# Finer decay steps, earlier decay-row loads and grouped state products in a hybrid DeltaNet/Mamba decoder step

## The chip, the cores and the metric

The kernel runs on one core of a Trainium2 chip. The metric is the device time of one execution in microseconds; the time before is the median of three runs. The engines are TensorE (PE, matmuls; PEld is its weight load), VectorE (DVE), ScalarE (ACT), GpSimd (POOL) and SyncE (SP, which here issues nearly all DMA transfers, in order).

## The reference

One step of a two-layer decoder trunk, for a prompt of 256 tokens and for 8 samples of 4 tokens each that carry states. Layer 0 mixes tokens by a gated DeltaNet, layer 1 by a Mamba-2 scan; each is followed by a SwiGLU network. Cut to what the change touches:

```python
def _gated_delta_rule(q, k, v, g, beta, s0):          # 16 heads of 128
    cum = jnp.cumsum(g, axis=-1)
    seg = cum[..., :, None] - cum[..., None, :]
    decay = jnp.exp(jnp.where(causal, seg, -jnp.inf))
    kk = jnp.einsum('bnhik,bnhjk->bnhij', kb, k) * decay
    tri = jnp.eye(c) + jnp.where(strict, kk, 0.0)
    sol = lax.linalg.triangular_solve(tri, rhs, left_side=True, lower=True, unit_diagonal=True)
    qk = jnp.einsum('bnhik,bnhjk->bnhij', q, k) * decay
    # per block: delta = u - w S;  o = (q e^cum) S + qk delta;  S = e^last S + k_dec^T delta

def _ssd_scan(x, dt, a, bm, cm, h0):                  # 32 heads of 64, 4 groups
    decay = jnp.exp(jnp.where(causal, seg, -jnp.inf))
    cb = jnp.einsum('bnigs,bnjgs->bnijg', cm, bm)
    y_diag = jnp.einsum('bnijg,bnijgr,bnjgrp->bnigrp', cb, decay, xdt)
```

The samples start from `s0 = state_gdn`, so that their k and q are multiplied with 8 x 16 state matrices of 128 x 128.

## The kernel before

All 288 tokens (256 of the prompt, 32 of the samples) lie along the free dimension of x, 128 model columns to a partition block. Every projection is a "dense pair" (`dense_g`, `dense_chunk`): weights of 128 x 1024 come in by one 512 KB DMA from SP into a tile of the tag `raw` (six buffers), ACT rounds them to `wh`, DVE takes the rest as `wl`, and PE multiplies three times (`pd<-hh,wh`, `pd<-hh,wl`, `pd<-hl,wh`). Work is written as generators that yield between steps. `weave` (a planner) takes several generators with a number of steps each and traces them in proportion; a scheduler then puts the instructions of every engine in order, earlier traced work first where it is ready, and each engine runs its own instructions strictly in that order. `burst` traces the first of a list of matmuls and puts the others right behind it at high priority.

The stages that matter here, in the order of time:

- *Decays* (function `gdn`, around L750). The cumulative decays of the prompt's 16 heads are written to DRAM (`cumd`, `cumq`) and read back, repeated over partitions. `D` holds the decays inside blocks of 32 tokens, 128 x 1024: four loads (L753), an add of `nb`, a clamp, one exponential. Behind this exponential, by `issue_after`, come `elS` and `cbs` (the samples' decays, 128 x 512, four clamps and an exponential). This is traced ahead of the first weave (L783), which runs the tasks `k0 q0 k1 k3 q1 k2 q2 q3`: the dense pairs for k and q with their convolutions, and the modulation's matmuls (`mods`). In a convolution, `hist` is a copy by ACT of a transposed piece of the old rows, `kf` is DVE's last step of one block of k. `D` is used only after this weave, when the blocks' triangular matrices are inverted.
- *State products* (`s0_products`, L720 to L743). DVE inverts the blocks in a series of 31 pairs of operations on `X`; beside it run the dense pairs of z and v and, for r = 0 and 1, the products of the samples' k and q (`kms`) with the states. Per batch there is one 512 KB load into a `raw` tile (`s0`, in the trace `s`) and four matmuls of 32 columns (`spa<-s,kms`) into one PSUM tile; the scheduler may put other matmuls between them. A float32 matmul is two instructions.
- *Head pairs* (`pre` and `scan`, L870 to L990). For each pair j of 16 heads, `pre(j)` builds the decays `PP` from `cumd` (two loads of 128 KB at L878, four clamped adds by DVE, an exponential by ACT) and the factors `U`, `Kd`; `scan(j)` runs the two blocks of 128 tokens: products `pe`, `pS`, `po2`, the last of which reads `PP` (`<-ep,PP`). `PP` has two buffers. One weave per pair holds `scan(j)`, `pre(j + 1)` and dense work; `sample` (with `KSQ`) is part of that dense list.
- *Mamba groups* (`core`, L1380 to L1425). Each group of 8 heads is done in four head pairs: DVE multiplies the decays `D` by the products of C and B, and four matmuls of 64 columns (`py<-D,xt`) give the pair's output; they are traced as plain matmuls.

Of the kernel before, what the change touches and what calls it, by code (L numbers as in the profile page):

```python
# [14 lines left out]
P = 128  # L15
# [3 lines left out]
NB = 8  # L19
# [8 lines left out]
def tile_hybrid_step(ctx: ExitStack, tc: tile.TileContext, I, O):  # L28
# [527 lines left out]
    def gdn(gt1, nrm):  # L556
# [165 lines left out]
        def s0_products(r, km):  # L722

            for h in range(2):
                for x_ in range(2):
                    o = 512 * h + 16 * (h if x_ == 0 else 1 - h)
                    G.tensor_copy(
                        km[:, o:o + 528].rearrange("p (b y) -> p b y", y=132)[:, :, 0:128].rearrange(  # L730
                            "p b (q t) -> p b q t", q=4)[:, :, :, 0:4],
                        kqs[:, r, x_, :, 16 * h:16 * h + 16].rearrange("p q (b t) -> p b q t", t=4))
            pa = pss.tile([P, 2, 256], F32, tag="s", name="spa")
            for b in range(NB):
                s0 = raw_tile("s0")
                SY.dma_start(s0.rearrange("p (h v) -> p h v", h=8),
                             I["state_gdn"][0, b, 8 * r:8 * r + 8].rearrange("h k v -> k h v"))
                for q in range(4):
                    mm(pa[32 * q:32 * q + 32, b // 4, :],
                       km[:, b * P + 32 * q:b * P + 32 * q + 32], s0[:, 256 * q:256 * q + 256],  # L740
                       start=(b == 0), stop=(b == NB - 1))
                yield
            cp(KSQ[:, r].rearrange("p x e v -> p x (e v)"), pa)  # L743

        with tc.tile_pool(name="gp1", bufs=1) as p1:
# [5 lines left out]
            D = v32(big("kt2", "D"))  # L751
            for b in range(4):
                SY.dma_start(D[32 * b:32 * b + 32], cumq[b].partition_broadcast(32))  # L753
            tt(D, D, nb.rearrange("p c h -> p (c h)").unsqueeze(2).to_broadcast([P, 32, 32]), ADD)
            ts(D, D, 0.0, None, MIN)
            eD = act(D, D, AF.Exp)
            with tc.issue_after(eD.ins):
                act(elS, cbs.rearrange("p i (q b t) -> p i q b t", q=4, t=4)[:, :, :, :, 3], AF.Exp)
                for i in range(4):
                    ts(cbs[:, i, :], cbs[:, i, :], nA[:, i:i + 1], 0.0, ADD, MIN)  # L760
                act(cbs, cbs, AF.Exp)

            def k_pair(p_):
                ps = []
# [16 lines left out]
                yield  # L781

            w1, n1 = plan("k0 q0 k1 k3 q1 k2 q2 q3", dict(k=(k_pair, 7), q=(q_pair, 5), z=(z_pair, 5), v=(v_pair, 7)))  # L783
            weave((w1, n1 + 1), (mods(8), 12))
            pk = pm([P, 2, P], "pks")
            for r in range(2):
                T.transpose(pk[:, r, :], ksr[:, 4 * r:4 * r + 4, :].rearrange("p q t -> p (q t)"), ident)
# [77 lines left out]
                mm(p[:, e, :], lz[e], v[:, e, :])  # L865
            return p

        pres = {}

        def pre(j):  # L870

            for b in range(4):
                s = slice(32 * b, 32 * b + 32)
                for t, src in ((yn, Ync), (yd, Ydc)):
                    G.tensor_copy(t[s, :, :, s], src[s].rearrange("p (c h) i -> p c h i", c=2)[:, :, 2 * j:2 * j + 2, :])
            PP, U, Kd = fac("PP"), fac("U"), fac("Kd")
            for e in range(2):
                SY.dma_start(PP[:, :, e, :], cumd[2 * j + e, :].rearrange("(c i) -> c i", c=2).partition_broadcast(P))  # L878
            for c in range(2):
                for e in range(2):  # L880
                    ts(PP[:, c, e, :], PP[:, c, e, :], nb[:, c, 2 * j + e:2 * j + e + 1], 0.0, ADD, MIN)
            act(PP, PP, AF.Exp)
            pres[j] = (PP, U, Kd)
            for c in range(2):
                pk = pm([P, 2, P], "pkk", "f")
                mm(pk, kq(c, j, 0), kqt[j][:, 2 * c * P:(2 * c + 2) * P])
                yield
                GM = p2.tile([P, 2, P], F32, tag="GM", name="GM", bufs=1)
                tt(GM, pk, mKQ, MUL)
                NN = p2.tile([P, 2, P], F32, tag="NN", name="NN", bufs=1)  # L890
                gx = lambda x: GM[:, x:x + 1, :].to_broadcast([P, 2, P])
                tt(NN, PP[:, c], gx(0), MUL)
                tt(PP[:, c], PP[:, c], gx(1), MUL)
                pt = pm([P, P], "pkt2", "m")
                T.transpose(pt, kq(c, j, 0), ident)
                for e in range(2):
                    h = 2 * j + e
                    act(Kd[:, c, e, :], pt, AF.Copy, scale=bte[:, c, h:h + 1])
                pz = pm([P, 2, P], "pz", "f")
                for e in range(2):  # L900
                    mm(pz[:, e, 0:96], NN[:, e, :], yn[:, c, e, 0:96])
                yield
                NY = NYs[c]
                cp(NY[:, :, 0:96], pz[:, :, 0:96])
                G.tensor_copy(U[:, c, :, 0:32], yd[:, c, :, 0:32])
                v = yd[:, c]
                for o in (32, 64, 96):
                    p = pm([P, 2, P], "pch", "f")
                    for e in range(2):
                        mm(p[:, e, o:], NY[:, e, :], v[:, e, o:])  # L910
                    yield
                    tt(U[:, c, :, o:], yd[:, c, :, o:], p[:, :, o:], SUB)
                    v = U[:, c]
                yield

        def scan(j):
# [6 lines left out]
            for c in range(2):  # L923
                if c == 1:
                    pq = pm([P, 2, P], "pkq", "m")
                    mm(pq, kq(1, j, 0), S1)
                    yield
                    for e in range(2):
                        stt(vt[:, 1, e, :], pq[:, e, :], hs_(ec, 1, e), vt[:, 1, e, :], MUL, ADD)
                p = two("pe", U[:, c], vt[:, c])  # L930
                yield
                ep = p2.tile([P, 2, P], F32, tag="ep", name="ep")
                cp(ep, p)
                pS = two("pS", Kd[:, c], ep)
                yield
                Sn = p2.tile([P, 2, P], F32, tag="S", name="Sn")
                if c == 0:
                    cp(Sn, pS)
                else:
                    for e in range(2):  # L940
                        stt(Sn[:, e, :], S1[:, e, :], el1[:, 2 * j + e:2 * j + e + 1], pS[:, e, :], MUL, ADD)
                    SY.dma_start(O[2][0, 0, 2 * j:2 * j + 2].rearrange("h k v -> k h v"), Sn)
                    pq2 = pm([P, 2, P], "pq2", "m")
                    mm(pq2, kq(1, j, 1), S1)
                    yield
                    qo = p2.tile([P, 2, P], F32, tag="qo", name="qo", bufs=1)
                    for e in range(2):
                        act(qo[:, e, :], pq2[:, e, :], AF.Copy, scale=hs_(ec, 0, e))
                po = two("po2", PP[:, c], ep)
                yield  # L950
                if c == 0:
                    cp(o[:, c], po)
                else:
                    tt(o[:, c], po, qo, ADD)
                for e in range(2):
                    act(junk, o[:, c, e, :], AF.Square, accum=oss[:, c, e:e + 1])
                S1 = Sn
                yield
# [104 lines left out]
        proj = out_proj(I["gdn_w_out"][0], ((0, 8), (8, 16)), 16, OV(0), OV(1), gt1, nrm)  # L1063

        run = lambda g: [None for _ in g]
        run(pre(0))
        fk = dict(v=(v_pair, 7), z=(z_pair, 5), m=(mods, 0), s=(sample, 9), p=(lambda n: take(proj, n), 0),
                  o=(lambda n: sample_out(n // 100, range(n // 10 % 10, n % 10)), 1))
# [135 lines left out]
    def ssm(gt1, nrm):  # L1204
# [181 lines left out]
        def core(g, pt="m"):  # L1386
# [8 lines left out]
            for pp in range(4):  # L1395
                D = Ds.pop((g, pp))
                tt(D, D, f2(CBm).unsqueeze(1).to_broadcast([P, 2, 384]), MUL)
                py = pm([P, NP_], "py", pt)
                for e in range(2):
                    s = slice(64 * e, 64 * e + 64)  # L1400
                    mm(py[s, :], xt[:, 0, pp, s], D[:, e, 0:256], stop=False)
                for e in range(2):
                    s = slice(64 * e, 64 * e + 64)
                    mm(py[s, P:], xt[:, 1, pp, s], D[:, e, 256:384], start=False)
                yield
                blk = 4 * g + pp
                stt(xf[:, pp, :], xf[:, pp, :], Dp[:, blk:blk + 1], py, MUL, ADD)
                tt(xf[:, pp, :], xf[:, pp, :], zfs[g, pp // 2][:, pp % 2, :], MUL)
                if pp == 0:
                    sq = sp.tile([P, NP_], F32, tag="sqa", name="sqa", bufs=1)  # L1410
                    act(sq, xf[:, pp, :], AF.Square)
                else:
                    s1 = sqt("ssq")[:, 0:NP_]
                    act(s1, xf[:, pp, :], AF.Square)
                    tt(sq, sq, s1, ADD)
                yield
# [378 lines left out]
```

## Time and profile before

| | |
|---|---|
| median of three runs | 1180.42 us (1175.89 to 1183.29) |
| the profiled execution's own time | 1180.71 us |
| its span in the profile | 1178.8 us |
| mean granted TensorE clock | 0.979 |
| largest group: three matmuls of each dense pair, `pd` | 56% of the chain that ended last |

The span runs from the first to the last instruction; what lies around it is 1.9 us. Busy time of PE is the time in which at least one matmul is in flight. A timeline row has start, length, engine, line, operation, the tiles (written <- read), the shape and the count, and in brackets the idle time of the engine just before with what ended it. Where several equal instructions follow each other, a row holds them all. Most lines are those of helpers (L62 is every matmul, L72, L75 and L78 are DVE's, L82 and L87 ACT's), so work is told apart by its tiles.

### The profile page before, as it was taken

What the parts mean: (1) busy time and instruction counts of PE and PEld (TensorE: products, weight loads), DVE (VectorE), ACT (ScalarE), POOL (GpSimd) and SP (SyncE); (2) the same over time, 40 slices, a digit from 0 to 9 for tenths busy, and PEclk for the clock granted to TensorE, in tenths of its full rate; (3) what the DMA queues carried; (4) which work ended last, traced back from release to release, by engine and by line L of the source; (5) the groups of instructions that cost most, each with busy time, mean ns of one, the idle gap of its engine ahead of it and who ended that gap; (6) DMA issues with size and microseconds to landing.
All of it is one profiled execution on the core that took longest, in us unless ns stands there. A gap on an engine that the chain in (4) does not pass through costs nothing.

```text
span 1178.8 us, 23230 instructions
## 1 busy us (share of the span) xinstructions
PE 1116.5 (95%) x8560; PEld 1020.2 (87%) x8560; DVE 853.6 (72%) x2095; ACT 617.0 (52%) x1317; POOL 124.7 (11%) x324
## 2 busy tenths in 40 slices
PE   5899999999999999999999999999999999999996
PEld 2688877798988969999999789778979899999996
DVE  2777897788967777666655597678987787666654
ACT  3578444555535474444433468779744574444432
POOL 3012113212100022010000111001000010000000
PEclk8899998999999999999999999999999999999999
DMA  8856597453454469988777657577575679887761
GB/s 300 255 183 196 165 278 244 157 154 92 134 166 145 152 220 318 294 271 270 246 220 228 222 169 238 172 212 240 175 234 178 218 214 283 254 247 229 224 212 43
DMA packets 270000, 249.04 MB, mean 211 GB/s; under 512 B 13314, under 2 KB 256247, under 8 KB 269888
## 3 DMA queue, kind: packets, MB, share of 16 engines
q1 hardware_dynamic: 269256, 247.51, 67.8%
q8 instruction: 67, 1.10, 0.4%
q14 instruction: 45, 0.37, 0.1%
q10 hardware_dynamic: 632, 0.07, 0.0%
HBM read 226.64 MB, written 20.90 MB: 210 GB/s over the span
## 4 chain that ended last, share of the span: by engine, by line
PE 73%; DVE 8%; ACT 5%; DMA 4%; issue 1%; POOL 1%; SPq 0%; DVEq 0%; ACTq 0%; POOLq 0%
PE pd L62 56%; PE pch L62 4%; DVE wl L75 2%; PE mod L62 2%; DVE cva L72 1%; DMA PP<-cumd 1%; DMA D<-scumd 1%; PE py L62 1%; ACT D L82 1%; ACT wh L87 1%; PE spa L62 1%; PE pht L1458 1%; DMA rw<-in_ssm_w_in_dram 1%; PE lu L62 1%; PE lsu L62 1%
## 5 line engine op out<-in xcount | busy, mean ns | idle before, releaser
L62 PE MATMUL pd<-hh,wh 128*128 128x288 f32 x1424 | 427.5, 303 | 12.5 <-ACT hh L87 9.1
L62 PE MATMUL pd<-hh,wl 128*128 128x288 f32 x1424 | 429.7, 302 | 3.9 <-DVE wl L75 3.9
L62 PE MATMUL pd<-hl,wh 128*128 128x288 f32 x1424 | 425.4, 300 | 0.0
L75 DVE TENSOR_TENSOR wl<-rw,wh 128x1024 fp32r<-128x1024 f32 (+2 forms) x258 | 311.2, 1206 | 145.2 <-PE pd L62 106.7
L87 ACT ACTIVATE wh<-rw 128x1024 fp32r<-128x1024 f32 (+2 forms) x258 | 268.3, 1042 | 240.8 <-PE pd L62 146.8
L62 PEld LDWEIGHTS pd<-hh,wh 128*128 128x128 f32 x1424 | 269.2, 190 | 26.4 <-issue 13.8
L62 PEld LDWEIGHTS pd<-hh,wl 128*128 128x128 f32 x1424 | 270.5, 190 | 10.1 <-DVE wl L75 5.9
L62 PEld LDWEIGHTS pd<-hl,wh 128*128 128x128 f32 x1424 | 270.8, 190 | 2.6 <-issue 1.6
L62 PE MATMUL pd<-ah,wh 128*128 128x288 f32 x352 | 104.6, 297 | 0.0
L62 PE MATMUL pd<-al,wh 128*128 128x288 f32 x352 | 104.5, 297 | 0.0
L62 PE MATMUL pd<-ah,wl 128*128 128x288 f32 x352 | 104.1, 296 | 0.0
L72 DVE SCALAR_TENSOR_TENSOR cva<-ext,vT,cva 128x312 f32<-128x312 f32 x168 | 86.1, 536 | 10.5 <-ACT cva L82 9.6
L62 PEld LDWEIGHTS pd<-ah,wl 128*128 128x128 f32 x352 | 66.3, 188 | 0.0
L62 PEld LDWEIGHTS pd<-ah,wh 128*128 128x128 f32 x352 | 66.1, 188 | 0.1
L62 PEld LDWEIGHTS pd<-al,wh 128*128 128x128 f32 x352 | 66.2, 188 | 0.0
L62 PE MATMUL mod<-wm,csT 128*32 128x256 f32 x704 | 52.8, 429 | 0.5 <-ACT csT L87 0.4
L495 POOL COPY cvo<-ext 128x27 f32<-128x27 f32 x56 | 22.9, 412 | 188.4 <-ACT ext L87 183.9
L72 DVE SCALAR_TENSOR_TENSOR h0u<-h0u,elP,lsu 128x128 f32<-128x128 f32 x128 | 36.0, 341 | 6.9 <-PE lsu L62 5.9
L72 DVE SCALAR_TENSOR_TENSOR s0u<-s0u,elS,lu 128x128 f32<-128x128 f32 x128 | 36.0, 340 | 6.5 <-PE lu L62 6.5
L62 PE MATMUL pd<-yh,wh 128*128 128x288 f32 x128 | 38.7, 302 | 1.2 <-ACT yh L87 1.2
L87 ACT ACTIVATE ext<-pd 128x256 f32<-128x256 f32 x112 | 27.6, 290 | 23.2 <-PE pd L62 20.8
L62 PE MATMUL pd<-ogh,wh 128*128 128x288 f32 x128 | 39.4, 308 | 0.0
(544 smaller groups left out, 1791.7 us busy)
## 6 DMA issues: line engine op xcount, KB each, us to landing
wm<-in_w_mod_dram SPq DMA_DIRECT2D x88, 512.0 KB
rw<-in_ffn_w_gate_up_dram SPq DMA_DIRECT2D x88, 512.0 KB
rw<-in_gdn_w_in_dram SPq DMA_DIRECT2D x48, 512.0 KB
rw<-in_ffn_w_down_dram SPq DMA_DIRECT2D x40, 512.0 KB
rw<-in_ssm_w_in_dram SPq DMA_DIRECT2D x40, 512.0 KB
s<-in_state_gdn_dram SPq DMA_DIRECT2D x16, 512.0 KB
rw<-in_gdn_w_out_dram SPq DMA_DIRECT2D x16, 512.0 KB
s0u<-in_state_gdn_dram SPq DMA_DIRECT2D x16, 512.0 KB
```

Of the source, the lines that this page charges most:

```text
L62: return T.matmul(out, lhsT=lhsT, rhs=rhs, start=start, stop=stop)
L72: return V.scalar_tensor_tensor(out=out, in0=a, scalar=s, in1=b, op0=o0, op1=o1)
L75: V.tensor_tensor(out=out, in0=a, in1=b, op=op)
L82: return S.activation(out=out, in_=a, func=f, bias=bias, scale=scale)
L87: S.activation(out=out, in_=a, func=AF.Copy)
L495: G.tensor_copy(o[:, c % 4, 0:27].rearrange("p (n s) -> p n s", s=3), e[:, 256:319].rearrange("p (n s) -> p n s", s=7)[:, :, 0:3])
L1458: T.transpose(pt[:, k, :], h0[:, o:o + P], ident)
```

## The change

Four edits, all in the order and the grouping of instructions; the arithmetic stays the same, apart from the order in which the two batches of a pair are summed.

1. `D`, `elS` and `cbs` are no longer done at once ahead of the first weave but by a generator, `decay_steps`, that joins it with nine steps: the add of one half (the rows of one block of 128 tokens, 128 x 512), its clamp and exponential, the same for the other half, then `elS` and two clamps of `cbs`, the two others, and the exponential of `cbs`. The order that `issue_after` gave is gone. The loads of `D` stay where they were.
2. The four matmuls of a batch in `s0_products` are traced only after every second batch, eight at a time through `burst`, the later batch first.
3. The two loads of `PP` move from `pre(j)` to a function `load_pp`. It is called for pairs 0 and 1 ahead of `pre(0)`, and for pair j + 2 in `scan(j)`, right behind `po2` of the second block. The tag keeps its two buffers.
4. The four `py` matmuls of a Mamba head pair go through `burst`.

```diff
+            ss_ = []
             for b in range(NB):
                 s0 = raw_tile("s0")
                 SY.dma_start(s0.rearrange("p (h v) -> p h v", h=8),
                              I["state_gdn"][0, b, 8 * r:8 * r + 8].rearrange("h k v -> k h v"))
-                for q in range(4):
-                    mm(pa[32 * q:32 * q + 32, b // 4, :],
-                       km[:, b * P + 32 * q:b * P + 32 * q + 32], s0[:, 256 * q:256 * q + 256],
-                       start=(b == 0), stop=(b == NB - 1))
+                ss_.append(s0)
+                if b % 2:
+                    burst([lambda q=q, b=b_: mm(pa[32 * q:32 * q + 32, b // 4, :], km[:, b * P + 32 * q:b * P + 32 * q + 32],
+                                                ss_[b][:, 256 * q:256 * q + 256], start=(b == 1), stop=(b == NB - 2))
+                           for b_ in (b, b - 1) for q in range(4)])
                 yield
...
-            tt(D, D, nb.rearrange("p c h -> p (c h)").unsqueeze(2).to_broadcast([P, 32, 32]), ADD)
-            ts(D, D, 0.0, None, MIN)
-            eD = act(D, D, AF.Exp)
-            with tc.issue_after(eD.ins):
+            def decay_steps():
+                nbv = nb.rearrange("p c h -> p (c h)")
+                for h in range(2):
+                    ns = slice(16 * h, 16 * h + 16)
+                    tt(D[:, ns], D[:, ns], nbv[:, ns].unsqueeze(2).to_broadcast([P, 16, 32]), ADD)
+                    yield
+                    ts(D[:, ns], D[:, ns], 0.0, None, MIN)
+                    act(D[:, ns], D[:, ns], AF.Exp)
+                    yield
                 act(elS, cbs.rearrange("p i (q b t) -> p i q b t", q=4, t=4)[:, :, :, :, 3], AF.Exp)
                 for i in range(4):
                     ts(cbs[:, i, :], cbs[:, i, :], nA[:, i:i + 1], 0.0, ADD, MIN)
+                    if i % 2:
+                        yield
                 act(cbs, cbs, AF.Exp)
+                yield
...
-            weave((w1, n1 + 1), (mods(8), 12))
+            weave((w1, n1 + 1), (mods(8), 12), (decay_steps(), 9))
...
+        def load_pp(j):
+            PP = pps[j] = fac("PP")
+            for e in range(2):
+                SY.dma_start(PP[:, :, e, :], cumd[2 * j + e, :].rearrange("(c i) -> c i", c=2).partition_broadcast(P))
...
-            PP, U, Kd = fac("PP"), fac("U"), fac("Kd")
-            for e in range(2):
-                SY.dma_start(PP[:, :, e, :], cumd[2 * j + e, :].rearrange("(c i) -> c i", c=2).partition_broadcast(P))
+            PP, U, Kd = pps.pop(j), fac("U"), fac("Kd")
...
                 po = two("po2", PP[:, c], ep)
+                if c and j < 6:
+                    load_pp(j + 2)
                 yield
...
+        load_pp(0)
+        load_pp(1)
         run(pre(0))
...
-                for e in range(2):
-                    s = slice(64 * e, 64 * e + 64)
-                    mm(py[s, :], xt[:, 0, pp, s], D[:, e, 0:256], stop=False)
-                for e in range(2):
-                    s = slice(64 * e, 64 * e + 64)
-                    mm(py[s, P:], xt[:, 1, pp, s], D[:, e, 256:384], start=False)
+                ev = lambda e: slice(64 * e, 64 * e + 64)
+                burst([lambda e=e: mm(py[ev(e), :], xt[:, 0, pp, ev(e)], D[:, e, 0:256], stop=False) for e in range(2)] +
+                      [lambda e=e: mm(py[ev(e), P:], xt[:, 1, pp, ev(e)], D[:, e, 256:384], start=False) for e in range(2)])
```

More of the change, by code (lines that the diff above doesn't have):

```diff
@@ L866, in apply_n @@
             return p
-        pres = {}
+        pres, pps = {}, {}
+        def load_pp(j):
+            PP = pps[j] = fac("PP")
+            for e in range(2):
+                SY.dma_start(PP[:, :, e, :], cumd[2 * j + e, :].rearrange("(c i) -> c i", c=2).partition_broadcast(P))
         def pre(j):
```

## The prediction

> **What bounds the kernel now.** I read the page first (shares, slices, chain), then the busy time in windows, then the timeline of each stretch that the change touches.
>
> ```profile
> span 1178.8 us, 23230 instructions
> PE 1116.5 (95%) x8560; PEld 1020.2 (87%) x8560; DVE 853.6 (72%) x2095; ACT 617.0 (52%) x1317; POOL 124.7 (11%) x324
> PE 73%; DVE 8%; ACT 5%; DMA 4%; issue 1%; POOL 1%; SPq 0%; DVEq 0%; ACTq 0%; POOLq 0%
> ...
> 70.00:82.00 12.00, 9.87 (x69) 8.32 (x68) 9.51 (x24) 7.84 (x24) 1.71 (x7) 0.86 0.29 91
> 140.00:190.00 50.00, 46.52 (x347) 36.39 (x345) 46.51 (x119) 17.26 (x35) 6.87 (x18) 0.93 0.91 275
> 700.00:900.00 200.00, 193.45 (x1491) 167.98 (x1490) 157.99 (x380) 142.76 (x318) 14.43 (x41) 1.00 0.70 214
> ```
>
> PE is busy 95% of the span and carries 73% of the chain, so only two things can give time back: PE idling (1178.8 - 1116.5 = 62 us over the whole span), and PE running below its rate. The window rows (PE, PEld, DVE, ACT, POOL, granted clock, DMA share, GB/s) place this for three of the four stretches that the edits touch: 2.1 us idle, at clock 0.86, at 70 to 82 (decays), 3.5 us at 140 to 190 (DeltaNet state products), 6.5 us at 700 to 900 (Mamba). The fourth, the scans from 190 to 420, is read below by its waits.
>
> **Edit 1: decays in small steps.** The block rows D (128 x 1024) are added, clamped and exponentiated whole; then elS, the four cbs clamps and the cbs exponential are ordered right behind.
>
> ```profile
> 76.06 0.44 PE L775 MATMUL pkt<-ident,kf 128*128 128x128 f32 x2 [0.77 <-DVE kf L72]
> 78.31 0.45 PE L459 MATMUL po<-ident,cvo 128*128 128x128 f32 x1 [1.28 <-ACT hist L87]
> 78.80 0.44 PE L62 MATMUL pd<-hl,wh 128*128 128x288 f32 x1
> ...
> 80.96 0.44 PE L62 MATMUL pd<-hl,wh 128*128 128x288 f32 x1
> ...
> 74.45 1.22 DVE L75 TENSOR_TENSOR D<-D,nb 128x1024 f32<-128x1024 f32 x1
> 75.59 0.42 DVE L72 SCALAR_TENSOR_TENSOR kf<-ext,cva 128x256 f32<-128x256 f32 x1
> 76.64 1.06 ACT L82 ACTIVATE D<-D 128x1024 f32<-128x1024 f32 x1 [0.31 <-DVE D L78]
> 77.61 0.42 ACT L82 ACTIVATE elS<-cbs 128x128 f32<-128x128 f32 x1
> 77.94 0.23 ACT L87 ACTIVATE hist<-ph 128x96 f32<-128x96 f32 x1
> ...
> L75 DVE TENSOR_TENSOR D<-D,Gd x2: 686/689/692, 139.4 to 140.0; 128x512 f32<-128x512 f32 x2
> L82 ACT ACTIVATE PP<-PP x8: 614/630/635, 196.3 to 349.8; 128x512 f32<-128x512 f32 x8
> ```
>
> The reader is to see PE wait twice: 0.77 us for kf, which stands behind the D add on DVE, and 1.28 us for hist, which stands behind the D exponential and elS on ACT. Right behind, the dense matmuls start 0.24 us apart (ten rows from 78.80 to 80.96) instead of 0.13 (161.10 to 161.23, in the next fence): 10 x 0.11 = 1.1 us more. Halves cost 2 x 0.69 - 1.22 = +0.16 on DVE and 2 x 0.63 - 1.06 = +0.20 on ACT; both engines have free time here (9.51 and 7.84 of 12 us). The seven steps are spread over slots 1 to 33 of 49. But the rows are first touched at 74.45, and the kf just behind belongs to the third of the eight tasks, slots 13 to 19, when four of the seven steps are due. So I expect the two halves close together near 74 to 78 us, and only elS and cbs really later. The hist wait then shrinks by half an exponential (0.43) and by elS (0.42): -0.85. The kf wait I leave, since one half still goes ahead of it. The slow rows I let go with the hist wait: -1.1. Sum -2.0. Ends: all of it, -0.77 - 1.28 - 1.1 = -3.15; nothing saved and both extras exposed, +0.4.
> [...]
>
> **Edit 2: DeltaNet state products of two batches as one group.** 64 products (two instructions each) no longer go four at a time but eight.
>
> ```profile
> 134.79 0.62 PE L62 MATMUL spa<-s,kms 128*32 128x256 f32 x2
> ...
> 161.10 0.29 PE L62 MATMUL pd<-hh,wl 128*128 128x288 f32 x1
> 161.23 0.29 PE L62 MATMUL pd<-hl,wh 128*128 128x288 f32 x1
> 161.45 0.64 PE L62 MATMUL spa<-s,kms 128*32 128x256 f32 x8
> 162.02 0.40 PE L62 MATMUL pd<-hh,wh 128*128 128x288 f32 x1
> ...
> 175.09 0.64 PE L62 MATMUL spa<-s,kms 128*32 128x256 f32 x8
> ...
> 82.82 0.29 PE L62 MATMUL pd<-hl,wh 128*128 128x288 f32 x1
> 83.05 1.07 PE L62 MATMUL mod<-wm,csT 128*32 128x256 f32 x16
> 84.05 0.53 PE L62 MATMUL pd<-hh,wh 128*128 128x288 f32 x2
> ...
> 179.15 0.43 DVE L72 SCALAR_TENSOR_TENSOR vf<-ext,cva 128x256 f32<-128x256 f32 x1 [0.99 <-ACT ext L82]
> DMA s<-in_state_gdn_dram: 0.7, 2
> ```
>
> From the start of the dense matmul before to that of the one after takes 0.79 us around eight instructions (161.23 to 162.02) and 1.23 around sixteen of the same shape (the modulation's, 82.82 to 84.05). So joining two eights saves 2 x 0.79 - 1.23 = 0.35 us. The trace has 16 such stretches from 134.79 to 175.09 (one a run of 30); eight groups of sixteen would free some 0.35 x 8 = 2.8 us of PE. But the window row shows DVE just as full as PE (46.51 against 46.52 of 50 us) with the inversion's long series, and the stage ends when that series ends. What PE frees, DVE can use only where it waits on PE's products: one wait, 0.99 us at 179.15. So -1.0; ends -2.8 (all) and +2.0, since the first tile of a pair now keeps one of six raw buffers until the second has landed, one 512 KB transfer at 275 GB/s (1.9 us) later.
>
> **Edit 3: decay rows a head pair ahead.** Two 128 KB loads for each pair are issued in the scan behind the last product that reads the old rows, no longer at the start of the next pair but one's preparation. There are still two PP buffers.
>
> ```profile
> 341.09 0.71 PE L62 MATMUL pq<-ep,PP 128*128 128x128 f32 x4
> 340.79 0.37 SPq L273 DMA_DIRECT2D rw<-in_gdn_w_out_dram  x1
> 341.83 0.88 SPq L878 DMA_DIRECT2D PP<-cumd  x2
> 347.87 0.29 DVE L78 TENSOR_SCALAR PP<-PP,nb 128x128 f32<-128x128 f32 x1 [2.08 <-DMA PP<-cumd]
> 349.36 0.68 PE L62 MATMUL pch<-KSQ,NNs 128*128 128x128 f32 x4 [2.43 <-DVE KSQ L72]
> ...
> 288.26 0.68 PE L62 MATMUL pch<-ep,PP 128*128 128x128 f32 x4
> 288.97 1.07 SPq L878 DMA_DIRECT2D PP<-cumd  x2
> ...
> DVE PP L78 <- DMA PP<-cumd: 4.4, 5, 2.1
> ```
>
> DVE waits 4.4 us for these rows, five times, and the worst wait holds KSQ up behind it: PE idles 2.43 us. But the loads already go out when the buffer comes free: the last reader ends at 341.80 and the load is issued at 341.83; at 288.94 and 288.97. Moving the statement up cannot pass that, because the data hazard is the same. So 0. Ends: -4.7 if every such wait went (PE's 2.43 us, and for the other four waits the 4.4 - 2.08 = 2.3 us that DVE loses), +1.0 if SP stands at the load while weight loads queue behind it (two loads took 1.07 us instead of 0.88).
>
> **Edit 4: the Mamba pair's products as a group.**
>
> ```profile
> 739.64 0.87 PE L62 MATMUL py<-D,xt 128*64 128x256 f32 x8
> 740.44 0.66 PE L1458 MATMUL pht<-ident,h 128*128 128x128 f32 x4
> ...
> 781.68 0.65 PE L62 MATMUL py<-D,xt 128*64 128x128 f32 x4
> 782.27 0.66 PE L1458 MATMUL pht<-ident,h 128*128 128x128 f32 x4
> ```
>
> Most of the 16 groups run whole already, 0.80 us from start to the next instruction. Three are torn apart, and the torn-off piece costs 0.59 more: 3 x 0.59 = 1.8 us. PE idles 6.5 of 200 us in this stretch, mostly waiting for ACT and DVE, so I take -1.0; ends -1.8 and 0.
>
> Sum: -2.0 - 1.0 + 0 - 1.0 = -4.0. The profiled execution took 1180.71 us, 0.3 above the median of 1180.42; I predict 1176.7.
>
> **The rivals.**
> 1. *Nothing moves (1178.5 to 1183).* What is freed turns into waiting elsewhere: DVE is as full as PE in the state products, and the halves still stand in front of hist. For it: the 46.51 us. Against it: the slow rows at 78.80.
> 2. *The PP loads get out ahead of weight loads (1170 to 1174).* A 512 KB weight load was issued at 340.79, 1.04 us ahead of the PP pair; placed behind it, the PP rows need not share the transfer, which at 275 GB/s is 1.9 us, about the 2.08 us that DVE waited. Then the waits of edit 3 go: 1176.7 - 4.7 = 1172.0. Against it: SP would have to stand idle until 341.8. [...]
> 3. *Slower: pairs starve the raw buffers (1181 to 1189).* Weights and state tiles share six buffers. At 140 to 190 the DMA engines are 0.91 busy. If four of the eight groups pass their 1.9 us on to the dense work behind, edit 2 costs +7.6 instead of -1.0: 1176.7 + 8.6 = 1185.3. It decides from the point where DVE waits for PE at the end of that stretch by more than the 0.99 us of now. Against it: PE's waits for state tiles come to 0.7 us now, in two places.
>
> **How the numbers follow.** The forecast's case (2 to 7 us gained) gets 0.50, rival 1 0.20, rival 2 0.13, rival 3 0.12; 0.05 is for a new order that moves more either way. The range takes in the sum with its ends, rival 1, most of rival 2 and the lower half of rival 3: 1168 to 1186. A difference of about 1% (11.8 us) is what this measurement tells from no change. Faster than 1168.6 needs rival 2 and the far ends of edits 1, 2 and 4 (1172.0 - 1.2 - 1.8 - 0.8 = 1168.2): 0.08. Slower than 1192.2 needs rival 3 beyond its price: 0.05. Within 1%: 0.87.
>
> **What would show it.** Edit 1: no dense rows 0.24 us apart near 80 us, hist earlier than 77.94. Edit 2: eight stretches of 16, DVE as full as before and its inversion ending at most 1 us sooner in its own stage. Edit 3: PP issues still right behind the last reader, DVE's wait for PP still near 4.4 us. Edit 4: sixteen whole groups. I am wrong if PP waits vanish (rival 2), or if PE waits for state tiles in pairs (rival 3).

## The result and the profile after

| kernel | median | range | runs | profiled execution | its span | mean granted clock |
|---|---|---|---|---|---|---|
| before | 1180.46 us | 1174.46 to 1183.50 | 19 | 1180.71 us | 1178.8 us | 0.979 |
| after | 1172.21 us | 1169.40 to 1176.27 | 19 | 1171.25 us | 1169.5 us | 0.985 |

The ratio is 0.9939, with a 95% interval of 0.9926 to 0.9951: 7.2 us less (5.8 to 8.7). The two medians are 8.3 us apart; here and below gains are taken from the ratio, which has the interval. The time lies within the range that was predicted and on the predicted side of 1%. But the sum had -4.0 us, and its own case (2 to 7 us gained) was just left: 1172.2 falls among the times that were written down for rival 2. The experiments below show that the terms behind the sum had the wrong sizes.

First the page of the kernel after: span, busy times, and the shares of the chain that ended last by engine.

```profile
span 1169.5 us, 23201 instructions
PE 1106.9 (95%) x8560; PEld 1014.8 (87%) x8560; DVE 853.8 (73%) x2097; ACT 616.3 (53%) x1318; POOL 125.6 (11%) x324
PE 73%; DVE 9%; DMA 9%; ACT 6%; issue 2%; POOL 0%; SPq 0%; ACTq 0%; DVEq 0%; POOLq 0%
```

The matmuls are as many as before (8560); PE is busy for 9.6 us less and idle for 0.3 us more. Next the same three windows as in the prediction (busy time of PE, PEld, DVE, ACT and POOL with counts, granted clock, DMA share, GB/s).

```profile
70.00:82.00 12.00, 10.08 (x69) 8.34 (x67) 9.43 (x23) 8.49 (x28) 1.44 (x5) 0.86 0.54 177
140.00:190.00 50.00, 43.77 (x343) 36.55 (x345) 45.73 (x119) 19.28 (x41) 8.83 (x21) 0.90 0.86 262
700.00:900.00 200.00, 190.19 (x1472) 166.36 (x1471) 155.22 (x377) 135.56 (x299) 12.50 (x36) 1.00 0.67 202
```

The first window is as it was: 1.9 us idle in place of 2.1, and the clock again 0.86. In the second, PE has gone from 46.52 to 43.77 us busy and DVE has not got fuller. Next the decay stretch, by PE's timeline.

```profile
73.97 0.44 PE L785 MATMUL pkt<-ident,kf 128*128 128x128 f32 x2 [0.79 <-DVE kf L72]
74.65 0.54 PE L62 MATMUL pd<-hh,wh 128*128 128x288 f32 x2 [0.24 <-ACT wh L87]
...
76.00 0.40 PE L62 MATMUL pd<-hh,wl 128*128 128x288 f32 x1 [0.70 <-DVE wl L75]
76.24 0.38 PE L62 MATMUL pd<-hl,wh 128*128 128x288 f32 x1
76.41 0.44 PE L62 MATMUL pd<-hh,wh 128*128 128x288 f32 x1
76.65 0.44 PE L62 MATMUL pd<-hh,wl 128*128 128x288 f32 x1
```

The 1.28 us wait for hist is gone, but waits for wh (0.24) and wl (0.70) have come, 0.94 us in all. The rows of wl, one half of the weight tile that PE needs next, show why. First DVE's and PE's rows in the kernel before, then DVE's in the kernel after:

```profile
77.08 1.22 DVE L75 TENSOR_TENSOR wl<-rw,wh 128x1024 fp32r<-128x1024 f32 x1
78.41 0.59 PE L62 MATMUL pd<-hh,wl 128*128 128x288 f32 x1
...
74.73 1.21 DVE L75 TENSOR_TENSOR wl<-rw,wh 128x1024 fp32r<-128x1024 f32 x1
```

In the kernel before, wl was done at 78.30 (77.08 + 1.22), just when the wait for hist ended (78.31). So in this order the dense work could not have gone on sooner, whenever hist came: the two waits ran side by side, and the profile names only one. In the kernel after, hist is early and wl (74.73 + 1.21 = 75.94) is what PE waits for. The dense matmuls behind are still 0.24 us apart. Last, the state products and the Mamba products: the first and the last of eight and of sixteen rows.

```profile
132.71 1.07 PE L62 MATMUL spa<-s,kms 128*32 128x256 f32 x16
...
169.78 1.07 PE L62 MATMUL spa<-s,kms 128*32 128x256 f32 x16
728.05 0.87 PE L62 MATMUL py<-D,xt 128*64 128x256 f32 x8
...
888.61 0.87 PE L62 MATMUL py<-D,xt 128*64 128x256 f32 x8
```

Both edits do what they say: eight stretches of sixteen instructions, sixteen whole py groups.

### The profile page after: what moved, and what is told of

Read it like the earlier page. It is cut to its first block, busy times and chain, and to the rows that moved or that the text cites. A ratio compares the mean times of both kernels' runs of the same rounds, so it can differ in the third digit from the quotient of the medians.

```text
span 1169.5 us, 23201 instructions
## 1 busy us (share of the span) xinstructions
PE 1106.9 (95%) x8560; PEld 1014.8 (87%) x8560; DVE 853.8 (73%) x2097; ACT 616.3 (53%) x1318; POOL 125.6 (11%) x324
## 4 chain that ended last, share of the span: by engine, by line
PE 73%; DVE 9%; DMA 9%; ACT 6%; issue 2%; POOL 0%; SPq 0%; ACTq 0%; DVEq 0%; POOLq 0%
PE pd L62 56%; PE pch L62 4%; DVE wl L75 3%; PE mod L62 2%; DMA rw<-in_gdn_w_in_dram 2%; DMA D<-scumd 2%; DVE cva L72 2%; ACT wh L87 1%; DMA rw<-in_ssm_w_in_dram 1%; ACT D L82 1%; DMA wm<-in_w_mod_dram 1%; PE py L62 1%; DMA xt<-in_x_sample_dram 1%; PE pkk L62 1%; PE lu L62 1%
## 5 line engine op out<-in xcount | busy, mean ns | idle before, releaser
L82 ACT ACTIVATE ext<-cva 128x312 f32<-128x312 f32 x56 | 25.7, 463 | 28.3 <-DVE cva L72 23.2
L62 PEld LDWEIGHTS mod<-wm,csT 128*32 128x32 f32 x704 | 20.3, 117 | 22.8 <-issue 9.9
L62 PE MATMUL pd<-ogh,wl 128*128 128x288 f32 x128 | 39.0, 307 | 0.0
```

The costliest lines, as they stand in the source:

```text
L62: return T.matmul(out, lhsT=lhsT, rhs=rhs, start=start, stop=stop)
L82: return S.activation(out=out, in_=a, func=f, bias=bias, scale=scale)
```

## The experiments

All were timed beside the kernel before on the same chip; the three groups ran on different chips, so ratios are compared and not times. Where nothing else is said, the edit is made to the kernel before.

| kernel | median (runs) | before beside it | ratio and 95% interval |
|---|---|---|---|
| edit 1 alone | 1181.52 (12) | 1181.40 | 0.9995 (0.9972 to 1.0017) |
| edit 2 alone | 1174.09 (7) | 1181.40 | 0.9935 (0.9910 to 0.9961) |
| edit 3 alone | 1181.06 (12) | 1181.40 | 0.9993 (0.9972 to 1.0015) |
| edit 4 alone | 1179.92 (12) | 1181.40 | 0.9986 (0.9965 to 1.0006) |
| edits 1, 3 and 4 | 1180.52 (12) | 1182.27 | 0.9991 (0.9968 to 1.0014) |
| pairs, not tied | 1182.87 (12) | 1182.27 | 1.0003 (0.9979 to 1.0026) |
| single batches, tied | 1179.64 (12) | 1182.27 | 0.9984 (0.9967 to 1.0001) |
| groups of four, tied | 1181.23 (12) | 1182.27 | 0.9995 (0.9976 to 1.0013) |
| weight load held back | 1179.69 (12) | 1181.23 | 0.9982 (0.9966 to 0.9997) |
| pairs, not tied, load held | 1179.87 (12) | 1181.23 | 0.9984 (0.9966 to 1.0002) |
| groups of four, load held | 1177.22 (5) | 1181.23 | 0.9962 (0.9949 to 0.9975) |
| edits 2 and 4 | 1175.07 (6) | 1181.23 | 0.9948 (0.9927 to 0.9968) |

**Each edit alone.**

Edit 1, the D block in halves and in steps beside the other work:

```diff
+            def decay_steps():
+                for h in range(2):
+                    ns = slice(16 * h, 16 * h + 16)
...
-            weave((w1, n1 + 1), (mods(8), 12))
+            weave((w1, n1 + 1), (mods(8), 12), (decay_steps(), 9))
```

> The kernel before with edit 1 alone (decay steps). Theory of the prediction: -2.0 us, the wait for hist and the slow dense rows near 80 us gone. Rival (from the trace of the changed kernel, where the stage from 62 to 124 us gained only 0.3 us): 0 to -0.5 us, new small waits take the place of the old ones. Third theory (each edit reshuffles the scheduler's order far from its own place): anything from -4 to +4 us, with gains or losses in stages that the edit doesn't touch.

Edit 2, the products after every second batch, tied:

```diff
+                if b % 2:
+                    burst([lambda q=q, b=b_: mm(pa[32 * q:32 * q + 32, b // 4, :], km[:, b * P + 32 * q:b * P + 32 * q + 32],
...
+                           for b_ in (b, b - 1) for q in range(4)])
```

> The kernel before with edit 2 alone (state products in groups of eight matmuls). Theory of the prediction: -1.0 us, since DVE's inversion bounds the stage. Rival from the trace of the changed kernel (the stage from 131 to 190 us ended about 2 us sooner): -2 us. Third theory (reshuffling): -4 to +4 us with changes in other stages.

Edit 3, the decay rows issued behind the last reader:

```diff
                 po = two("po2", PP[:, c], ep)
+                if c and j < 6:
+                    load_pp(j + 2)
```

> The kernel before with edit 3 alone (decay rows a head pair ahead). Theory of the prediction: 0, since the loads go out at the same moment as before, when the buffer comes free. Rival: -4 to -6 us in the stretch from 190 to 410 us, which in the changed kernel ended some 6 us sooner; the DVE wait for the rows falls from 4.4 us to about 2. Third theory (reshuffling): -4 to +4 us with changes in other stages.

Edit 4, the four py products tied:

```diff
+                burst([lambda e=e: mm(py[ev(e), :], xt[:, 0, pp, ev(e)], D[:, e, 0:256], stop=False) for e in range(2)] +
+                      [lambda e=e: mm(py[ev(e), P:], xt[:, 1, pp, ev(e)], D[:, e, 256:384], start=False) for e in range(2)])
```

> The kernel before with edit 4 alone (Mamba products as groups). Theory of the prediction: -1.0 us between 700 and 900 us, nothing elsewhere. Rival: 0 or a small loss, since in the changed kernel that stretch gave back some 2 us.

Edit 2 alone gives 0.9935, as much as the whole change (0.9939), and more than any of the three theories had for it, though the third, a new order in other stages, is what the stages below show. Edits 1 and 3 give nothing that can be measured. Edit 4 gives -1.7 us by its ratio, with an interval that takes in both zero and the -1.0 that was expected.

**The other three together, and edit 2 with edit 4.** The kernel after with edit 2 undone (the diff of edit 2 reversed), and the kernel before with the diffs of edits 2 and 4.

> The kernel after with edit 2 undone: edits 1, 3 and 4 together. If the edits add up, the sum of the three alone, 0 + 0 - 1.5: 1178 to 1182 beside 1181 before. If another edit has its gain only together with the others, clearly less than 1178.

> Edits 2 and 4 alone, without the decay steps and the early decay-row loads. If edits 1 and 3 are worth nothing, also together with edit 2: 1172 to 1174 beside 1181.5, as the kernel after. If the kernel after needs them (the last PP wait is gone there and 0.8 us with edit 2 alone): 1174 to 1176.

Without edit 2 the rest is worth 0.9991, with an interval that takes in 1. With edits 2 and 4 alone it is 0.9948, whose interval overlaps that of the whole change; its 1175.1 lies in the bracket of the theory that the kernel after needs edits 1 and 3 too, but six runs cannot tell the two theories apart. So the gain is edit 2's in the main, and the question is why it is worth some 7 us and not the 1.0 of the prediction.

**What edit 2 is made of: place, tie and size.** Three variants of the products. As ordinary matmuls after every second batch:

```diff
+                if b % 2:
+                    for b_ in (b, b - 1):
+                        for q in range(4):
+                            mm(pa[32 * q:32 * q + 32, b_ // 4, :], km[:, b_ * P + 32 * q:b_ * P + 32 * q + 32],
```

> The kernel before with the state products traced after every second batch, eight in a row (the later batch first) but as ordinary matmuls: nothing ties them together or lifts them ahead of other work. Known so far: edit 2 alone gives 1174 against 1181. Theory A (pairing removes array switches, 0.35 us for each of eight joined pairs): 1178.5 to 1181, since the planner may tear the eights apart again. Theory B (the place in the trace counts: with the products one batch later the planner builds another order for what follows, and the first scan's chain starts some 2.5 to 3 us sooner): 1173 to 1176, first VectorE Sn about 23 us behind Ydc, as with edit 2. Theory C (the tie and the priority count, not the pairing): 1180 to 1182, no change.

Four tied products after each batch:

```diff
-                for q in range(4):
-                    mm(pa[32 * q:32 * q + 32, b // 4, :],
+                burst([lambda q=q, b=b, s0=s0: mm(pa[32 * q:32 * q + 32, b // 4, :], km[:, b * P + 32 * q:b * P + 32 * q + 32],
...
+                       for q in range(4)])
```

> The kernel before with the four products of each single batch tied together with high priority; no pairing, same place in the trace. Theory A (array switches): 16 stretches of eight instructions as before, so 1180 to 1182. Theory B (place in the trace): no change either, 1180 to 1182, first VectorE Sn 25 to 27 us behind Ydc. Theory C (tie and priority): most of the gain of edit 2, 1173 to 1176.

Sixteen tied products after every fourth batch:

```diff
-                if b % 2:
+                if b % 4 == 3:
...
-                           for b_ in (b, b - 1) for q in range(4)])
+                           for b_ in (b, b - 1, b - 2, b - 3) for q in range(4)])
```

> The kernel before with the products of four batches as one tied group of sixteen products: four groups in place of edit 2's eight. Theory A (array switches): four switches fewer than with edit 2 at 0.35 us each, 1172 to 1174 unless a group has to wait for its four tiles. Theory B (place in the trace): another order again; no more gain than edit 2's, 1173 to 1181, and the first VectorE Sn says which. The rival on the raw buffers (four of six held until the last tile has landed): 1178 to 1189, with waits of TensorE for weight loads or for state tiles between 130 and 190 us.

None of the three comes near edit 2. In the variant without the tie the profile has ten stretches of products, five of them sixteen instructions long, and the ratio is 1.0003; its first VectorE Sn comes 24.8 us behind Ydc (207.69 and 182.90), where theory B wanted 23. With groups of four there are just four stretches of 32, and the ratio is 0.9995. With tied single batches the first Sn comes even sooner, 21.9 us behind Ydc, and the ratio is 0.9984. The theory of array switches (0.79 us around eight instructions and 1.23 around sixteen, in the rows of the prediction), in which fewer are always better, has fallen as the main cause, and so has theory C, by which tied single batches should have had most of the gain. That the first scan starts sooner, theory B's sign, is not enough either, and it is not needed: with edits 2 and 4 the first Sn comes 24.6 us behind Ydc, as late as without the tie. Only pairs and tie together have the gain.

So I went by stages. These window rows cut the kernel before at four marks: the start of the last row of pkb (131.23), the end of the inversion (first write of Ydc, 185.43), the first update of a state in a scan (DVE's first Sn, 212.53), the last output of the scans (start of the last ogh, 391.03); the last window ends at the first ld of the FFN behind (428.98).

```profile
131.23:185.43 54.20, 50.69 (x400) 38.13 (x399) 48.34 (x134) 18.70 (x44) 7.89 (x20) 0.95 0.82 245
185.43:212.53 27.10, 26.96 (x201) 24.91 (x200) 17.51 (x39) 14.51 (x36) 12.12 (x35) 0.97 0.61 195
212.53:391.03 178.50, 171.17 (x1306) 154.19 (x1306) 143.94 (x489) 89.16 (x254) 24.88 (x73) 0.97 0.45 145
391.03:428.98 37.95, 35.61 (x281) 31.64 (x280) 30.10 (x75) 20.83 (x33) 6.48 (x17) 0.96 0.69 217
```

The same marks in the kernel with edit 2 alone:

```profile
130.37:184.13 53.76, 48.52 (x407) 38.88 (x405) 48.29 (x136) 19.32 (x45) 9.32 (x20) 0.94 0.85 253
184.13:207.06 22.93, 21.63 (x167) 19.51 (x166) 15.92 (x36) 12.29 (x31) 12.32 (x35) 1.00 0.58 195
207.06:386.40 179.34, 175.31 (x1350) 157.00 (x1349) 146.79 (x493) 91.91 (x262) 25.89 (x73) 0.98 0.48 150
386.40:422.60 36.20, 33.70 (x266) 29.22 (x264) 28.88 (x72) 19.63 (x33) 6.50 (x17) 0.95 0.69 217
```

And in the kernel after:

```profile
129.25:182.72 53.47, 47.24 (x396) 37.99 (x396) 47.52 (x134) 18.09 (x42) 8.44 (x18) 0.93 0.85 255
182.72:206.13 23.41, 23.41 (x173) 21.50 (x172) 15.61 (x37) 12.82 (x32) 11.66 (x35) 0.94 0.56 188
206.13:382.47 176.34, 172.48 (x1350) 155.79 (x1349) 146.89 (x493) 91.69 (x262) 24.75 (x73) 1.00 0.48 152
382.47:418.68 36.21, 33.68 (x265) 29.56 (x264) 28.87 (x72) 19.62 (x33) 6.48 (x17) 0.95 0.69 217
```

The reader is to see two things. In the inversion PE is busy for 2.2 us less (50.69 and 48.52) and idle for 1.7 more (54.20 - 50.69 = 3.51, and 53.76 - 48.52 = 5.24): the stage is only 0.44 us shorter, as an engine beside it sets its end (DVE, busy for 48.34 and 48.29 us). Behind the inversion, 30 or so fewer PE instructions stand ahead of the first state update (201 and 167), which so comes 4 us sooner; they fill the scans instead (1306 and 1350), where PE's idle time falls from 7.33 to 4.03 us, and 15 fewer are left behind the scans (281 and 266), which takes 1.75 us off there. These counts alone are not the gain: edit 1 alone has 156 and 1336, and it gained nothing.

A single profile has a few microseconds of its own: the kernel with edit 4 alone has the same DeltaNet program as the kernel before, and from the first mark to the last it took 294.61 us against 297.75. So I take means. In five profiles without edit 2 (before, edits 1, 3 and 4 alone, and those three together) the inversion's stage takes 54.18 us with 3.80 idle, and from its end to the last mark 242.06 us with 11.19 idle. In three with edit 2 (alone, with edit 4, after) it is 53.63 with 5.54, and 237.98 with 8.20. So edit 2 gains 0.55 us in the inversion and 4.1 us behind it, and 3.0 of the 4.1 are idle time of PE that is gone. The five lie between 240.4 and 243.7 us behind the inversion, the three between 236.0 and 239.5, so the 4.1 is good to a few microseconds only.

**Where that idle time was.** In the profiles of all eight kernels without edit 2's gain one wait in the scans stands out, at the last head pair's decay rows: PE stands 1.8 to 3.4 us there, and DVE 1.2 to 3.2 at its longest. In the five kernels without edit 2 it is 3.07 us in the mean, as much as the 3.0 of idle time that edit 2 takes away. The kernel with edit 4 alone shows it as the kernel before does (rows of SP's queue, DVE and PE). DVE's two rows are the first uses of what the first and the second of the two loads bring:

```profile
335.45 0.37 SPq L273 DMA_DIRECT2D rw<-in_gdn_w_out_dram  x1
336.49 0.88 SPq L878 DMA_DIRECT2D PP<-cumd  x2
339.95 0.29 DVE L78 TENSOR_SCALAR PP<-PP,nb 128x128 f32<-128x128 f32 x1 [0.25 <-DMA PP<-cumd]
343.52 0.29 DVE L78 TENSOR_SCALAR PP<-PP,nb 128x128 f32<-128x128 f32 x1 [3.21 <-DMA PP<-cumd]
345.00 0.68 PE L62 MATMUL pch<-KSQ,NNs 128*128 128x128 f32 x4 [3.42 <-DVE KSQ L72]
```

In the kernel with edit 2 alone the queue has the other order:

```profile
336.96 0.88 SPq L880 DMA_DIRECT2D PP<-cumd  x2
338.23 0.37 SPq L273 DMA_DIRECT2D rw<-in_gdn_w_out_dram  x1
...
340.83 0.60 PE L62 MATMUL pch<-KSQ,NNs 128*128 128x128 f32 x4
...
340.67 0.28 DVE L78 TENSOR_SCALAR PP<-PP,nb 128x128 f32<-128x128 f32 x1
341.82 0.28 DVE L78 TENSOR_SCALAR PP<-PP,nb 128x128 f32<-128x128 f32 x1 [0.80 <-DMA PP<-cumd]
```

With the 512 KB weight load ahead, the second load's rows come 7.0 us behind the first issue (336.49 to 343.52), DVE stands 3.21 us and PE 3.42. With the rows ahead it is 4.9 us (336.96 to 341.82), DVE stands 0.80, and PE does not wait, since KSQ is done before DVE gets to the rows. The first load's rows are no later with the weight load ahead: 3.5 us behind the issue (336.49 to 339.95), and at most 3.7 in the other order. So two things differ: the order of SP's queue, and DVE's order, in which KSQ now stands ahead of the rows. The second alone is not enough, for the pairs without a tie have KSQ ahead of the rows too, and PE stands 2.93 us behind them, for U. Nothing in edit 2 speaks of these loads: the planner, given other products some 170 us earlier, places them otherwise.

**That one order, put right by hand.** The load may go out only behind the last pair's rows:

```diff
+        held = W is late_w[0] and (c0, k0) == late_w[1]          # gdn_w_out, columns 512, rows 0
+        with tc.issue_after(late_w[2].ins) if held else ExitStack():
+            SY.dma_start(r[:, :n].rearrange("p (k c) -> p k c", c=256),
...
-                SY.dma_start(PP[:, :, e, :], cumd[2 * j + e, :].rearrange("(c i) -> c i", c=2).partition_broadcast(P))
+                late_w[2] = SY.dma_start(PP[:, :, e, :], cumd[2 * j + e, :].rearrange("(c i) -> c i", c=2).partition_broadcast(P))
```

> The kernel before with one load held back: the out-projection's weight tile (columns 512, rows 0) may be issued only behind the last head pair's decay rows. In the profiles of all eight kernels without edit 2's gain that 512 KB load goes out 1.04 us ahead of the last PP pair, VectorE then waits 1.6 to 3.2 us for the rows, and TensorE 1.8 to 3.4 us behind it; in the two kernels with the gain it goes out behind and that wait is 0.8 us or none. Theory D (this one order is a main part of edit 2's gain): no TensorE wait over 1 us near 345, and 1178 to 1179 beside 1181.5, 2.4 to 3.4 us faster. Theory E (edit 2's gain is the fewer array switches): no change in time, the idle of TensorE turns up elsewhere in the scans.

The same edit on the pairs without a tie, and on the groups of four:

> State products in pairs as ordinary matmuls, with the same weight load held behind the last decay rows. Its products already run mostly in eights (ten stretches against sixteen), and without the hold it gained nothing (1182.9 beside 1182.3). Theory D: 1179 to 1180, and TensorE's wait of 2.9 us for U behind the PP rows is gone. If switches and this order together are edit 2's gain: 1175 to 1178. Theory E: no change from 1182.

> Groups of four batches with the same weight load held behind the last decay rows. Theory D together with the switches saved: 1178 beside 1181 for the groups of four without the hold; TensorE's wait of 2.2 us for KSQ is gone. The waits for state tiles in the inversion (7.7 us of TensorE idle there against 5.2 with pairs) stay, so it doesn't reach edit 2's 1174. Theory E: it should already have been the fastest of all, which it was not; no change.

The kernel with the load held, in its rows of SP's queue, DVE, ACT and PE:

```profile
341.16 0.88 SPq L882 DMA_DIRECT2D PP<-cumd  x2
342.09 0.47 SPq L277 DMA_DIRECT2D rw<-in_gdn_w_out_dram  x1
...
344.59 0.29 DVE L78 TENSOR_SCALAR PP<-PP,nb 128x128 f32<-128x128 f32 x1 [0.62 <-DMA PP<-cumd]
...
346.35 0.29 DVE L78 TENSOR_SCALAR PP<-PP,nb 128x128 f32<-128x128 f32 x1
...
347.94 1.06 ACT L87 ACTIVATE wh<-rw 128x1024 fp32r<-128x1024 f32 x1 [1.48 <-DMA rw<-in_gdn_w_out_dram]
348.90 0.35 ACT L82 ACTIVATE KSQ<-spq,ec 128x128 f32<-128x128 f32 x1
...
346.15 0.68 PE L62 MATMUL pch<-KSQ,NNs 128*128 128x128 f32 x4 [0.55 <-DVE KSQ L72]
349.30 0.66 PE L62 MATMUL pch<-U,NY 128*128 128x64 f32 x4 [1.41 <-ACT KSQ L82]
```

The wait for KSQ falls to 0.55 us as theory D has it, but 1.41 us come back three microseconds later, for ACT: its split of the weight tile (347.94) now waits 1.48 us for that load, and in ACT's order it stands ahead of the second half of KSQ. DVE's order has moved too (KSQ now stands between its first and its second use of the rows), so this is not one order alone. The time falls by 0.18% (0.03 to 0.34), 2.1 us: somewhat less than D's 2.4 to 3.4. On the pairs without a tie the ratio goes from 1.0003 to 0.9984, with intervals that overlap. On the groups of four it goes from 0.9995 to 0.9962, and those intervals do not: 3.9 us. Theory E, by which the order is worth nothing, has fallen; theory D holds for a part. The pairs without a tie were to reach 1175 to 1178 if fewer stretches and this order together were edit 2's gain; they came to 1179.9, though in their profile PE's work lies as with edit 2 (1350 instructions in the scans, 265 behind). So the two together are not all of it. No kernel here is measurably faster than the kernel after.

Groups of four pay in the inversion, where PE is busy as little as with edit 2 but the stage is longer:

```profile
131.75:187.95 56.20, 48.55 (x399) 40.68 (x398) 48.31 (x133) 19.71 (x45) 7.39 (x20) 0.91 0.79 236
```

Its idle time is 56.20 - 48.55 = 7.65 us. The list of what PE waited for in that window (total, times, longest) begins:

```profile
PE pd L62 <- DVE wl L75: 2.1, 3, 1.6
PE pd L62 <- ACT wh L87: 2.0, 1, 2.0
```

So 4.1 us of it are spent on weight tiles that are not split yet, and none on state tiles, of which the expectation for the groups of four with the load held speaks. Waits of this kind are there in smaller size elsewhere: 2.7 us in the kernel after, 0.3 with edit 2 alone, 1.6 before. Dense work that is starved because four of six raw buffers are held by one group would look like this, as in rival 3 of the prediction; that the buffers are the cause was not tested by itself.

## Why the prediction came out as it did

**The total came within the range by luck.** -4.0 us was predicted and -7.2 came; the terms were -2.0, -1.0, 0 and -1.0, and the ratios of one edit at a time put -0.6, -7.7, -0.8 and -1.7 beside them, of which the first, the third and the fourth cannot be told from 0. Two us that did not come in edit 1 made up for part of the six that edit 2 brought beyond its term. (The 1176.7 is the sum taken from the profiled execution; from the median it would be 1176.4.)

**Edit 2 is the step that failed: a term of -1.0, where about 7 us came.** Its argument for its own stage was right in the main. 2.8 us of PE time by eight joined pairs was the price, 2.2 us were freed, and the stage's end moved by 0.4 to 0.7 us, because DVE, busy for 48.3 us of it before and with edit 2 alone, sets it; PE idles instead, 3.7 us of it for DVE's vf with edit 2 alone and 1.2 before. The -1.0 itself rested on a wrong reading: the 0.99 us at 179.15 is by its row a wait for ACT's ext, which stands behind two weight splits on ACT, and not for a product of PE. What failed was to end the sum at the end of the stage. The planner orders some 1800 matmul instructions behind the inversion anew, and there the order came out better: by 4.1 us in the means of the profiles. The one piece that was tried by itself, the place of a weight load, is worth 2.1 us alone (0.4 to 4.0), with a new wait on ACT that edit 2 does not have. The prediction gave 0.05 to "a new order that moves more either way", and that is the case that occurred.

What stays open: the profiles place 4.6 us of edit 2's gain of some 7. That is all by which the profiled executions differ: the five without edit 2 took 1179.0 us in the mean and the three with it 1174.5, at nearly the same granted clock (0.983 and 0.982). Over all timed runs the mean granted clock is 0.983 with edit 2 and 0.979 to 0.980 in the kernel before, and among the runs of the kernel before 0.001 of clock goes with some 0.8 us. By an estimate from these numbers (3 x 0.8) that is the rest, but whether the clock is cause or effect was not tested. No run gives a price to the fewer instructions ahead of the first state update by themselves. The pairs without a tie had them too (172 in that window, 1337 in the scans), and gained nothing.

**Rival 2 had a good part of the mechanism, at the wrong edit.** The weight load at 340.79 that rides ahead of the rows costs, and its price, PE's 2.43 us, is near the 2.1 measured. In the kernel after, the order is turned round and DVE waits 2.1 us for rows where it waited 4.4, so the sign for rival 2 came half true, through edit 2. But edit 3 cannot move it, and did not: its ratio alone is 0.9993, and in its profile the weight load still goes out 1.04 us ahead of the last rows (335.52 and 336.56), and DVE waits 5.2 us for rows. So the 0 for edit 3 was right, by its reason. How the time of the rows goes with the order of SP's queue shows beside the held load: the second load's rows are used 5.2 us behind the first issue, without a wait, when the weight load is held (341.16 to 346.35), and 6.0 before, with one (341.83 to 347.87). But the first load's rows come 3.4 us behind their issue with the load held (341.16 to 344.59) and 3.6 before (341.83 to 345.44), so the weight load ahead hardly delays these. Why it is the second that comes late stays open.

**Edit 1 was mis-sized: -2.0, and nothing that can be told from 0 was measured (-0.6, from -3.3 to +2.0).** Two of its steps fell. The wait for hist went, as it should, but it was not the one that ended last: wl of the next weight tile was not ready before 78.30 anyway, and waits for that tile's halves took its place, 0.24 + 0.70 us against 1.28. And the 1.1 us of slow rows were never that wait's. The same wait of 1.28 us (1.27 with edit 4 alone) stands in the eleven profiles without edit 1. The window row of the four microseconds from its end in the kernel before:

```profile
78.31:82.31 4.00, 4.00 (x21) 4.00 (x22) 1.76 (x7) 2.04 (x6) 1.25 (x5) 0.62 0.07 17
```

And in the kernel with edit 4 alone, whose program is the same up to there:

```profile
78.39:82.39 4.00, 4.00 (x37) 3.61 (x41) 2.77 (x9) 3.31 (x9) 1.14 (x5) 1.00 0.06 15
```

One has clock 0.62 and 21 matmuls, the other 1.00 and 37. Of the eleven, six have 0.57 to 0.62 and five have 1.00; with edit 1 it is 0.57 once (after) and 1.00 twice. So the slow rows belong to an execution and not to the program, and no edit may be credited with them on the strength of one profile. In the kernel before, PE has no longer wait ahead of the slow rows from 60 us on (1.28 us for hist, then 0.77 for kf), and in the five the clock stays at 1.00 behind the same wait. So this wait by itself does not set the clock, and what does was not shown.

**Edit 4's -1.0 is neither shown nor refuted by the time,** -1.7 with an interval from -4.1 to +0.7; but its own stretch gained nothing in the profiles. From the start of the last lu row to the first lsu (627.42 to 960.22 in the kernel before) the four kernels with edit 4 take 334.3 us in the mean and the ten without it 334.2. PE idles 17.4 us there in place of 15.0. So the torn groups were joined, all sixteen of them, PE was freed of some 2.4 us, and this turned into waiting, as rival 1 has it.

**Rival 3 did not occur with pairs.** PE's idle time in the inversion rose from 3.5 to 5.2 us, but the stage ended sooner, and PE waits for no state tile. (The prediction's 0.7 us of such waits counts PE's weight load too; PE itself waited 0.2.) With groups of four it does look that way (56.20 us in place of 54.20), but for weight tiles.

## What to carry to other kernels

Where a planner orders the work, an edit's own stage is only half of its price: look up what the new order does to the loads and to the filler work of the following stages, and say openly that a bound on the stage does not bound the sum. A wait that recurs in every variant without the gain and is missing in those with it can be tested by putting that order right by hand, which here took a few lines and gave 2 us without the edit. A profile names one wait at a time: before a wait is put down as a gain, ask when the next thing that the engine needs will be there. And a stretch of slow rows in one profile is no property of the program until a second execution of the same code shows it.

## What the runs showed of the hardware

The granted clock differs from one execution to the next at one and the same place: 0.57 to 0.62 or 1.00 behind the same wait, in six and five profiles, with 19 to 21 matmul instructions in the four microseconds or with 37. By an estimate from these rows a drop of that kind costs up to 4.00 x (1 - 0.57) = 1.7 us. The mean clock of a whole execution goes with its time, loosely: in the 19 runs of the kernel after, those at 0.977 took 1175.8 and 1176.3 us, the profiled one at 0.985 1171.3, but one at 0.981 took 1169.7. Differences of two or three microseconds between two single profiles are therefore no evidence; equal counts and recurring waits are.
